# Keeping the low parts of one set of FFN weights in DRAM, made early, in a two-layer recurrent decoder on one core

## The chip, the cores and the metric

The kernel runs on one core of one Trainium2 chip. The metric is the device time of one execution in microseconds (us). The engines are named as in the profile: PE (TensorE matmul), PEld (its weight load, which overlaps the matmuls), DVE (VectorE), ACT (ScalarE), POOL (GpSimd) and SP (SyncE, which here issues nearly all DMAs, in order).

## The reference, cut to what matters

Two layers, each `x = x + mixer(rmsnorm(x))` and then `x = x + swiglu(rmsnorm(x))`, over 1024 prompt rows and 64 sample rows (1088 columns in the kernel). Layer 0's mixer joins an S5 recurrence and a gated delta network, layer 1's mixer is RWKV-7. The change touches the SwiGLU of layer 1 only, with d = 1024 and 2816 hidden columns (22 blocks of 128):

```
def swiglu(h, w_gate, w_up, w_down):
    return (jax.nn.silu(h @ w_gate) * (h @ w_up)) @ w_down
```

Everything is float32. The kernel gets close to float32 from three faster products: a weight `w` is split into a rounded high part `wh` and a low part `wl = w - wh`, the activation likewise into `hi` and `lo`, and each block computes `wh*hi + wh*lo + wl*hi` (helper `mm`, line 322).

## The kernel before

The columns are worked in two halves (512 and 576 columns), and each half in two chunks (256 or 288 columns). The program is written as: projections and recurrences of layer 0; then for each half layer 0's output projection and FFN 0, followed by the RWKV projections and the RWKV units (eight feature tiles, two time segments each) of that half; then for each half layer 1's output projection and FFN 1. A list scheduler reorders it, engine by engine, so that work from neighbouring stages is interleaved: the RWKV units of the first half run beside FFN 0 of the second half, and the RWKV units of the second half run beside FFN 1 of the first half. The FFN 1 of the second half has nothing beside it.

An FFN (`ffn`) goes through 22 hidden blocks. For each block it makes the gate product and the up product (PSUM tiles `pg`, 24 matmuls for a chunk, two PSUM banks in turn), forms the activation (`s`, `ah`, `al`: lines 510 to 519) and, for every three blocks, runs the down product: eight output tiles, each two chunks of nine matmuls into `pd`, which DVE adds to the residual (line 534). The next output tile needs a new 128x384 weight.

Every weight comes through the helper `weight` (lines 295 to 312 of the listing below): SP loads it from DRAM into one of two `raw` buffers, ACT rounds it into `wh` (line 305), and the low part is made by a subtraction (line 309) on POOL, or on DVE where the caller says so. The FFN's down weights use DVE in the stages that have no RWKV beside them (`alone`). A weight of class `Kept` is different: the first time its low part is also stored to a DRAM copy (line 311), and from then on (`there`) the low part is loaded (line 307) and no subtraction is made. Before the change the layer-0 FFN weights and the projections are `Kept`; the layer-1 FFN weights `wg`, `wup` and `wd` are not, so that FFN 1 makes its low parts twice, once for each half.

The pools that matter: `raw` has two buffers, `wh` and `wl` three, `wdh` and `wdl` two. Memory on the right side of the scratchpad is first layer 0's and, after `right.close()`, that of the RWKV constants and work tiles.

Of the kernel before, what the change touches and what calls it, by code (L numbers as in the profile page):

```python
# [8 lines left out]
F32 = mybir.dt.float32  # L9
F32R = mybir.dt.float32r  # L10
# [15 lines left out]
NF = D_FF // 128  # L26
# [78 lines left out]
class Kern:  # L105
# [188 lines left out]
    def weight(self, src, kt=8, m=128, tag="w", bufs=3, lo=None):  # L294


        nc = self.nc
        kept, src = (src, src.src) if isinstance(src, Kept) else (None, src)
        raw = self.dp.tile([128, 1024], F32, tag="raw", name="raw", bufs=2)
        raw = raw[:, :kt * m].rearrange("p (k m) -> p k m", m=m)  # L300
        nc.sync.dma_start(raw, src)
        p = self.dx if tag == "wd" else self.dp
        wh = p.tile([128, kt, m], F32R, tag=tag + "h", name=tag + "h", bufs=bufs)
        wl = p.tile([128, kt, m], F32R, tag=tag + "l", name=tag + "l", bufs=bufs)
        nc.scalar.copy(wh, raw)  # L305
        if kept and kept.root.there:
            nc.sync.dma_start(wl.bitcast(F32), kept.low)
            return wh, wl
        (lo or nc.gpsimd).tensor_sub(wl, raw, wh)  # L309
        if kept:  # L310
            nc.sync.dma_start(kept.low, wl.bitcast(F32))
        return wh, wl

    def mm(self, ps, w, x, cn, c=0):

        his, los = x
        wt = [[a[:, k] for k in range(len(his))] if not isinstance(a, list) else a for a in w]
        last = 3 * len(his) - 1
        i = 0
        for k, (xh, xl) in enumerate(zip(his, los)):  # L320
            for a, b in ((wt[0], xh), (wt[0], xl), (wt[1], xh)):
                self.nc.tensor.matmul(ps, a[k], b[:, c:c + cn], start=i == 0, stop=i == last)  # L322
                i += 1
# [1557 lines left out]
def mixed0(K, s, dyg, dy, wglu):  # L1881


    nc = K.nc
    v = nc.vector
    t0, W, chunks = HALF[s]
    kn = W // 8
    cn = 4 * kn
    gs = [K.hilo(4) for i in range(2)]
    ys = []  # L1890
    for m in range(4):
        t = K.ring("act", "yg")[:, :W]
        nc.sync.dma_start(t.rearrange("p (s k) -> p s k", s=8), dyg[m][:, :, 64 * s:64 * s + kn])
        ys.append(t)
        for i, (gh, gl) in enumerate(gs):
            y = t[:, cn * i:cn * i + cn]
            nc.scalar.activation(gh[m][:, :cn], y, AF.Copy, scale=0.5)
            v.scalar_tensor_tensor(gl[m][:, :cn], y, 0.5, gh[m][:, :cn], op0=OP.mult, op1=OP.subtract)
    hs = [([], []), ([], [])]
    for m in range(4):  # L1900
        w = K.weight(wglu[m], 4)
        for a in hs:
            h, l = K.hilo(1)
            a[0].extend(h)
            a[1].extend(l)
        for i in range(2):
            ps = K.pa("pgl")[:, :cn]
            K.mm(ps, w, gs[i], cn)
            t = K.tmp("gt")[:, :cn]
            nc.scalar.activation(t, ps, AF.Tanh, scale=0.5)  # L1910
            v.scalar_tensor_tensor(t, t, 1.0, ys[m][:, cn * i:cn * i + cn], op0=OP.add, op1=OP.mult)
            t3 = t.rearrange("p (s k) -> p k s", k=kn)
            for c in range(2):
                tc = t3[:, kn // 2 * c:kn // 2 * (c + 1)]
                oh, ol = (x[m][:, :cn].rearrange("p (k s) -> p k s", s=8)[:, :, 4 * i:4 * i + 4] for x in hs[c])
                nc.scalar.activation(oh, tc, AF.Copy, scale=0.25)
                v.scalar_tensor_tensor(ol, tc, 0.25, oh, op0=OP.mult, op1=OP.subtract)
    return [tuple(a + b for a, b in zip(x, y)) for x, y in zip(hs, loaded(K, s, dy))]


def loaded(K, s, dy, own=None):

    t0, W, chunks = HALF[s]
    hs = [([], []) for c in chunks]
    for i, y in enumerate(dy):
        t = K.ring("act", "yr")[:, :W]
        e = own is not None and i == len(dy) - 1
        n = W - own.shape[-1] if e else W
        K.nc.sync.dma_start(t[:, :n], y[:, t0:t0 + n])
        for (c, cn), (h, l) in zip(chunks, hs):  # L1930
            (a,), (b,) = K.hilo(1)
            m = min(max(n - c, 0), cn)
            if m:
                K.split(a[:, :m], b[:, :m], t[:, c:c + m], K.nc.gpsimd if i % 2 else None)
            if m < cn:
                K.split(a[:, m:cn], b[:, m:cn], own[:, c + m - n:c + cn - n])
            h.append(a)
            l.append(b)
    return hs


ORDER = ((0, 1), (2, 3))


@with_exitstack
def trunk(ctx, tc, *aps):
    nc = tc.nc
    I = dict(zip(IN_NAMES, aps))
    I.update({"o_" + n: a for (n, _), a in zip(OUTS, aps[len(IN_NAMES):])})
    K = Kern(ctx, tc)  # L1950
    K.nv = K.const.tile([128, 4, 8], F32, name="nv")
    dr = ctx.enter_context(tc.tile_pool(name="tkd", bufs=1, space=DRAM))
    dx = dr.tile([128, 8, T], F32, name="dx")
    dyr = [dr.tile([128, T], F32, name="dyr%d" % i) for i in range(8)]

    both = ["wglu", "wout", "w1", "a1", "g1", "wk", "wr", "wv", "wo"]
    for n in both:
        I[n] = Kept(I[n], dr.tile(list(I[n].shape), F32, name="low_" + n))
    for n in ("wg", "wup", "wd"):
        I[n] = [Kept(I[n][0], dr.tile(list(I[n].shape[1:]), F32, name="low_" + n)), I[n][1]]  # L1960
    right = ctx.enter_context(ExitStack())
    dyg, dy, second, early = layer0(K, I, right, dr)
    K.open(ctx, 288, 4, reuse_waits="tile")

    def tail(s, src, ys, w, i, x=None, done=None, ahead=lambda: None):
        if early is not None and s == i == 0:
            early.close()
            K.open_more(ctx, reuse_waits="tile")
        x = K.load_x(src, s, x)
        first = s == i == 0  # L1970
        ready = {}

        def gate():
            ready[0, 0] = K.weight(I["wg"][i][0])

        norms = K.project(x, ys, HALF[s][2], w, (lambda: None) if first else gate, 7 if first else 8)
        if first:
            second(ORDER[0])
            with tc.high_priority(3000):
                norms = K.project_last(x, ys, HALF[s][2], w, gate)  # L1980
            second(ORDER[1])
        return x, K.ffn(x, s, norms, K.nv[:, 1 + i], I["wg"][i], I["wup"][i], I["wd"][i], ready, ahead, s == i, done)

    rw = None
    for s in range(2):
        t0, W, chunks = HALF[s]
        wk0 = []
        keys = lambda: wk0.append(K.weight(I["wk"][0]))
        keep = lambda m, c, cn, t: nc.sync.dma_start(dx[:, m, t0 + c:t0 + c + cn], t)
        x, norms = tail(s, I["x"], mixed0(K, s, dyg, dy, I["wglu"]), I["wout"], 0, done=keep, ahead=keys)  # L1990
        if rw is None:
            right.close()
            rw = RWKV(K, ctx, I["rvec"])
            rw.open(ctx)
        unit = lambda ft, si=2 * s: rw.start(ft, si, I["rs0"], I["o_rwkv"], dyr)
        rw.projections(s, x, I["rsh"], *(I[n] for n in ("w1", "a1", "g1", "lw2", "wk", "wr", "wv")), unit, norms, wk0[0])
        for ft in range(8):
            own = unit(ft, 2 * s + 1)
        for w in [I[n] for n in both[:-1]] + [I[n][0] for n in ("wg", "wup", "wd")]:
            w.there = True  # L2000
    nc.sync.dma_start(I["o_shift"], rw.shift)
    for s in range(2):
        t0, W, chunks = HALF[s]
        I["wo"].there = s > 0
        if s:
            K.psn = rw.norm_bank
        x, (bc, r1) = tail(s, dx, loaded(K, s, dyr, own if s else None), I["wo"], 1, rw.spare() if s else None)
        with tc.issue_after(K.last.ins) if s else ExitStack():
            for i, (c, cn) in enumerate(chunks):
                K.rms([t[:, c:c + cn] for t in x], K.nv[:, 3], K.spread(r1) if i else bc,  # L2010
                      lambda k, t: nc.sync.dma_start(I["o_y"][:, k, t0 + c:t0 + c + cn], t), True,
                      ((1, 3, 5, 7), (5, 7))[i] if s else ())
# [95 lines left out]
```

## Time and profile before

| | us |
|---|---|
| median of three runs | 3722.46 (3709.42 to 3722.55) |
| the profiled execution, its own time | 3726.54 |
| its span in the profile | 3724.8 |
| PE busy | 3456.1 (93%) |
| DVE busy | 2377.6 (64%) |
| ACT busy | 1393.8 (37%) |
| POOL busy | 1041.9 (28%) |
| mean granted TensorE clock | 0.944 |

Busy times are unions of an engine's instructions. Matmuls overlap (one of 256 columns is shown with some 0.28 us, and the next starts 0.12 us later), so a busy PE only says that a matmul was under way. A wait is put down to what ended it. The profile's rows call the stages by time: FFN 0 of the first half runs to about 1100 us, FFN 0 of the second half from 1455 to 2130, FFN 1 of the first half from 2440 to 3200, and FFN 1 of the second half from 3225 to 3700.

### The profile page before, as it was taken

To read this page: it belongs to the slowest core of one execution; us is meant where nothing else is said; L and a number is where in the kernel's file an instruction comes from. 1 tells how busy PE (TensorE), PEld (TensorE's weight loads), DVE (VectorE), ACT (ScalarE), POOL (GpSimd) and SP (SyncE) were. 2 spreads that over 40 slices of the span, in tenths; PEclk is the share of its full clock that TensorE was granted. 3 is DMA by queue.
4 is the path that set the end of the run, shared out by engine and by line. 5 is a ranking of instruction groups with operands and counts; after the bars stand their busy time and mean duration, and the time that the engine had idled before them with its cause. 6 is when DMAs were issued, how large, how long until landed. Compare 5 with 4: busy or idle time off the path is not lost. (4 is left out here: it accounts for less than half of the span.)

```text
span 3724.8 us, 77416 instructions
## 1 busy us (share of the span) xinstructions
PE 3456.1 (93%) x29894; PEld 3211.8 (86%) x29894; DVE 2377.6 (64%) x6834; ACT 1393.8 (37%) x3264; POOL 1041.9 (28%) x1037
## 2 busy tenths in 40 slices
PE   7889999999998889999999988899999999899998
PEld 6879888899987788899999887888888878899997
DVE  6976888654456456766666663467787877453444
ACT  3333333322224444444444344444344433322222
POOL 3322233222316441211111042233343333132221
PEclk8989987999997899899999989999999999999999
DMA  4424453445554584344443435832233322522322
GB/s 102 96 84 129 96 176 93 143 144 174 188 173 125 172 275 149 110 142 141 140 151 117 137 117 176 281 127 60 81 94 93 91 70 84 179 74 72 94 80 66
DMA packets 387552, 474.36 MB, mean 127 GB/s; under 512 B 142312, under 2 KB 305896, under 8 KB 387184
## 3 DMA queue, kind: packets, MB, share of 16 engines
q1 hardware_dynamic: 377968, 460.51, 40.5%
q10 hardware_dynamic: 9216, 8.92, 0.7%
q8 instruction: 235, 3.85, 0.4%
q14 instruction: 133, 1.09, 0.1%
HBM read 344.32 MB, written 123.79 MB: 126 GB/s over the span
## 5 line engine op out<-in xcount | busy, mean ns | idle before, releaser
L322 PE MATMUL pg<-hi,wh 128*128 128x288 f32 (+1 forms) x2816 | 836.2, 297 | 17.8 <-DVE s L511 14.6
L322 PE MATMUL pg<-lo,wh 128*128 128x288 f32 (+1 forms) x2816 | 833.4, 296 | 5.7 <-DVE lo L409 4.7
L322 PE MATMUL pg<-hi,wl 128*128 128x288 f32 (+1 forms) x2816 | 831.5, 295 | 1.1 <-POOL wl L309 1.0
L309 POOL TENSOR_TENSOR wl<-raw,wh 128x1024 fp32r<-128x1024 f32 (+3 forms) x205 | 480.4, 2347 | 924.0 <-ACT wh L305 864.6
L322 PEld LDWEIGHTS pg<-hi,wh 128*128 128x128 f32 x2816 | 540.4, 192 | 29.8 <-DVE s L511 17.6
L322 PEld LDWEIGHTS pg<-lo,wh 128*128 128x128 f32 x2816 | 540.7, 192 | 13.5 <-DVE lo L409 6.3
L322 PEld LDWEIGHTS pg<-hi,wl 128*128 128x128 f32 x2816 | 540.7, 192 | 5.4 <-POOL wl L309 1.5
L305 ACT CAST wh<-raw 128x1024 fp32r<-128x1024 f32 (+3 forms) x309 | 312.8, 1013 | 394.6 <-PE pg L322 88.0
L322 PE MATMUL pd<-ah,wdh 128*128 128x256 f32 (+1 forms) x1280 | 385.2, 301 | 20.8 <-DVE x L534 15.1
L322 PE MATMUL pd<-ah,wdl 128*128 128x256 f32 (+1 forms) x1280 | 370.6, 290 | 0.6 <-DMA wdl<-low_wd 0.4
L322 PE MATMUL pd<-al,wdh 128*128 128x256 f32 (+1 forms) x1280 | 369.9, 289 | 0.0
L322 PEld LDWEIGHTS pd<-ah,wdh 128*128 128x128 f32 x1280 | 241.6, 189 | 30.6 <-DVE x L534 17.2
L322 PE MATMUL pj<-hi,wh 128*128 128x256 f32 (+1 forms) x768 | 243.3, 319 | 21.0 <-ACT st L1400 10.1
L322 PE MATMUL pj<-lo,wh 128*128 128x256 f32 (+1 forms) x768 | 243.2, 317 | 15.1 <-DVE lo L409 12.8
L322 PE MATMUL pj<-hi,wl 128*128 128x256 f32 (+1 forms) x768 | 238.5, 313 | 11.4 <-DMA wl<-low_wr 6.9
L322 PEld LDWEIGHTS pd<-ah,wdl 128*128 128x128 f32 x1280 | 241.5, 189 | 3.4 <-DMA wdl<-low_wd 1.3
L322 PEld LDWEIGHTS pd<-al,wdh 128*128 128x128 f32 x1280 | 242.0, 189 | 0.6
L534 DVE TENSOR_TENSOR x<-x,pd 128x256 f32<-128x256 f32 (+1 forms) x384 | 162.8, 427 | 96.3 <-PE pd L322 92.5
L305 ACT CAST wdh<-raw 128x384 fp32r<-128x384 f32 (+1 forms) x224 | 111.2, 497 | 258.4 <-PE pd L322 161.2
L322 PE MATMUL pi<-hi,wh 128*128 128x272 f32 x640 | 191.5, 299 | 3.1 <-ACT us L1809 1.5
L322 PE MATMUL pi<-lo,wh 128*128 128x272 f32 x640 | 190.4, 297 | 0.0
L322 PE MATMUL pi<-hi,wl 128*128 128x272 f32 x640 | 190.1, 297 | 0.0
(643 smaller groups left out, 8066.3 us busy)
## 6 DMA issues: line engine op xcount, KB each, us to landing
raw<-in_wg SPq DMA_DIRECT2D x88, 512.0 KB
raw<-in_wup SPq DMA_DIRECT2D x88, 512.0 KB
raw<-in_wd SPq DMA_DIRECT2D x192, 192.0 KB
low_wg<-wl SPq DMA_DIRECT2D x22, 512.0 KB
low_wup<-wl SPq DMA_DIRECT2D x22, 512.0 KB
wl<-low_wg SPq DMA_DIRECT2D x22, 512.0 KB
wl<-low_wup SPq DMA_DIRECT2D x22, 512.0 KB
raw<-in_win SPq DMA_DIRECT2D x20, 512.0 KB
```

The lines of the kernel that those rows point to most:

```text
L305: nc.scalar.copy(wh, raw)
L309: (lo or nc.gpsimd).tensor_sub(wl, raw, wh)
L322: self.nc.tensor.matmul(ps, a[k], b[:, c:c + cn], start=i == 0, stop=i == last)
L534: v.tensor_add(x[m][:, c:c + cn], x[m][:, c:c + cn], ps)
```

## The change

The gate weights of layer 1 (`wg`, 22 tiles of 128x1024, 512 KB each) become `Kept` too. A new helper `keep` goes through them once: it loads a tile into `kraw`, rounds it on ACT into `kwh`, subtracts on DVE into `kwl`, and stores `kwl` to DRAM. It uses one buffer of each kind, from a pool on the right side that is open between layer 0's close and the opening of the RWKV pools, and it stands in the program behind FFN 0 of the first half. FFN 1 then loads `wl` for its gate weights in both halves. Up and down weights of layer 1 stay as they are.

```diff
+    def keep(self, pool, w, n):
+
+        nc = self.nc
+        for i in range(n):
+            raw, wh, wl = (pool.tile(list(w[i].src.shape), t, tag=n, name=n, bufs=1)
+                           for n, t in (("kraw", F32), ("kwh", F32R), ("kwl", F32R)))
+            nc.sync.dma_start(raw, w[i].src)
+            nc.scalar.copy(wh, raw)
+            nc.vector.tensor_sub(wl, raw, wh)
+            nc.sync.dma_start(w[i].low, wl.bitcast(F32))
+        w.there = True
...
+FIRST = ('wg',)
...
     for n in ("wg", "wup", "wd"):
-        I[n] = [Kept(I[n][0], dr.tile(list(I[n].shape[1:]), F32, name="low_" + n)), I[n][1]]
+        I[n] = [Kept(I[n][i], dr.tile(list(I[n].shape[1:]), F32, name="low%d_%s" % (i, n)))
+                if i == 0 or n in FIRST else I[n][i] for i in range(2)]
...
         if rw is None:
             right.close()
+            with tc.tile_pool(name="keep", bufs=1, side="right") as kp:
+                for n in FIRST:
+                    K.keep(kp, I[n][1], NF)
             rw = RWKV(K, ctx, I["rvec"])
             rw.open(ctx)
```

In all the built program has 22 more loads (`kraw`), 22 more stores (`kwl`) and 44 more loads (`wl<-low_wg`) on SP, 22 more casts on ACT, 22 more subtractions on DVE and 44 fewer subtractions on POOL; the matmuls are the same in number.

Where `keep` goes is seen on DVE, in FFN 0 of the first half, at a down product. Before (an `x` row is the addition of a `pd` chunk to the residual, `wdl` the low part of a down weight):

```order
L519 SCALAR_TENSOR_TENSOR al<-s,ah 128x256
L534 TENSOR_TENSOR x<-x,pd 128x256 x2
L309 TENSOR_TENSOR wdl<-raw,wdh 128x384
L534 TENSOR_TENSOR x<-x,pd 128x256 x2
L309 TENSOR_TENSOR wdl<-raw,wdh 128x384
L534 TENSOR_TENSOR x<-x,pd 128x256 x2
L309 TENSOR_TENSOR wdl<-raw,wdh 128x384
L534 TENSOR_TENSOR x<-x,pd 128x256 x2
L309 TENSOR_TENSOR wdl<-raw,wdh 128x384
```

The same place now (line 546 is what was line 534, and 531 what was 519):

```order
L322 TENSOR_TENSOR kwl<-kraw,kwh 128x1024
L531 SCALAR_TENSOR_TENSOR al<-s,ah 128x256
L546 TENSOR_TENSOR x<-x,pd 128x256 x2
L309 TENSOR_TENSOR wdl<-raw,wdh 128x384
L546 TENSOR_TENSOR x<-x,pd 128x256 x2
L309 TENSOR_TENSOR wdl<-raw,wdh 128x384
L546 TENSOR_TENSOR x<-x,pd 128x256 x2
L322 TENSOR_TENSOR kwl<-kraw,kwh 128x1024
L309 TENSOR_TENSOR wdl<-raw,wdh 128x384
L546 TENSOR_TENSOR x<-x,pd 128x256 x2
```

Three new subtractions stand between this row of `al` and the end of this down product. Of the 22, seven stand among or right behind the additions of a down product and fifteen among the gate and up products; the first stands beside what ran at 851 us before, the last beside 1026 us.

On SP, at the same place, a row of before:

```order
L301 DMA raw<-in_wd 128x384
L311 DMA low_wd<-wdl 128x384
L301 DMA raw<-in_wd 128x384
L311 DMA low_wd<-wdl 128x384
L301 DMA raw<-in_wd 128x384
L311 DMA low_wd<-wdl 128x384
L301 DMA raw<-in_wd 128x384
```

And now:

```order
L301 DMA raw<-in_wd 128x384
L323 DMA low_wg<-kwl 128x1024
L320 DMA kraw<-in_wg 128x1024
L311 DMA low_wd<-wdl 128x384
L301 DMA raw<-in_wd 128x384
L311 DMA low_wd<-wdl 128x384
L301 DMA raw<-in_wd 128x384
L323 DMA low_wg<-kwl 128x1024
L320 DMA kraw<-in_wg 128x1024
```

A store that waits for DVE and a load of 512 KB come in for every two loads of a down weight. The loads of the RWKV constants (`rvec`), which stood right behind layer 0, now stand behind the last `kwl` store, as their memory is the pool's.

On POOL, at the start of FFN 1 of the first half, before (`yc`, `AR`, `BK`, `XV`, `H`, `Hs` belong to the RWKV units):

```order
L1713 TENSOR_TENSOR yc<-yc,rs 128x256
L309 TENSOR_TENSOR wl<-raw,wh 128x1024 x4
L1601 TENSOR_TENSOR AR<-rkb,P 64x4x64
L309 TENSOR_TENSOR wl<-raw,wh 128x1024
L1693 COPY Hs<-H 128x64
L1669 COPY XV<-Hs 64x64 x2
L1667 COPY H<-Hs 128x64
L309 TENSOR_TENSOR wdl<-raw,wdh 128x384
L1609 TENSOR_TENSOR BK<-kp,Pi 64x4x64 x2
L309 TENSOR_TENSOR wl<-raw,wh 128x1024
```

And now:

```order
L1725 TENSOR_TENSOR yc<-yc,rs 128x256
L309 TENSOR_TENSOR wl<-raw,wh 128x1024 x2
L1613 TENSOR_TENSOR AR<-rkb,P 64x4x64
L309 TENSOR_TENSOR wl<-raw,wh 128x1024
L309 TENSOR_TENSOR wdl<-raw,wdh 128x384
L1705 COPY Hs<-H 128x64
L1681 COPY XV<-Hs 64x64 x2
L1679 COPY H<-Hs 128x64
L309 TENSOR_TENSOR wdl<-raw,wdh 128x384
L1621 TENSOR_TENSOR BK<-kp,Pi 64x4x64 x2
```

Two of the four subtractions are gone there; what is left in FFN 1 are those of the up and down weights. The scheduler has also moved other instructions against each other in all stages where an FFN and RWKV units are interleaved; each pair of units still ends within some 85 of the FFN's matmuls from where it ended before.

## Rows read from the trace of the kernel before

**Rows 1.** The page's first part: engine, busy us, share of the span, instructions.
```profile
PE 3456.1 (93%) x29894; PEld 3211.8 (86%) x29894; DVE 2377.6 (64%) x6834; ACT 1393.8 (37%) x3264; POOL 1041.9 (28%) x1037
```

**Rows 2.** Busy time by stretch: length, PE, PEld, DVE, ACT, POOL, clock, DMA share, GB/s.
```profile
1455.00:2130.00 675.00, 666.17 (x6138) 612.05 (x6141) 442.59 (x1609) 281.13 (x738) 75.31 (x132) 0.98 0.44 132
2440.00:3200.00 760.00, 705.58 (x7135) 627.15 (x7135) 595.88 (x1858) 312.87 (x852) 273.86 (x262) 0.96 0.31 93
3225.00:3700.00 475.00, 465.53 (x3571) 459.73 (x3569) 200.04 (x380) 124.80 (x219) 112.80 (x52) 0.98 0.25 78
```

**Rows 3.** PE's waits in 2440 to 3200: us in total, times, longest.
```profile
PE pd L322 <- DVE x L534: 12.2, 14, 4.6
PE pg L322 <- DVE s L511: 9.5, 9, 1.9
PE pc L1678 <- ACT X L1677: 7.2, 5, 2.9
```

**Rows 4.** POOL's weight subtractions in 2440 to 3200 by shape: busy us, mean ns.
```profile
L309 POOL TENSOR_TENSOR wl<-raw,wh 128x1024 fp32r<-128x1024 f32 x48 | 115.5, 2410 | 123.1 <-ACT wh L305 110.5 <-PE po L322 4.4 <-PE pc L1678 2.3
L309 POOL TENSOR_TENSOR wdl<-raw,wdh 128x384 fp32r<-128x384 f32 x48 | 50.0, 1043 | 91.5 <-ACT wdh L305 77.8 <-DMA k<-dk 6.2 <-DMA raw<-in_wd 2.5
L309 POOL TENSOR_TENSOR wdl<-raw,wdh 128x256 fp32r<-128x256 f32 x8 | 5.8, 730 | 29.9 <-PE py L1689 15.8 <-ACT wdh L305 12.5 <-PE pd L322 1.6
```

**Rows 5.** Tile T in 1455 to 2130, then in 2440 to 3200: ns min/median/max.
```profile
L188 DVE TENSOR_TENSOR T<-T,Tm x210: 153/196/723, 1468.8 to 2067.4; 32x15 f32<-32x15 f32 x14, 32x39 f32<-32x39 f32 x14, 32x55 f32<-32x55 f32 x14, 32x63 f32<-32x63 f32 x14
L188 DVE TENSOR_TENSOR T<-T,Tm x225: 154/201/2432, 2440.0 to 3131.0; 32x15 f32<-32x15 f32 x8, 32x39 f32<-32x39 f32 x8, 32x55 f32<-32x55 f32 x8, 32x63 f32<-32x63 f32 x8
```

**Rows 6.** Order of time, 895 to 901, DVE and POOL: start, us, instruction.
```profile
898.92 2.40 DVE L519 SCALAR_TENSOR_TENSOR al<-s,ah 128x256 fp32r<-128x256 f32 x1 [0.90 <-ACT ah L518]
...
898.65 2.40 POOL L309 TENSOR_TENSOR wl<-raw,wh 128x1024 fp32r<-128x1024 f32 x1 [0.46 <-ACT wh L305]
```

**Rows 7.** Busy time by stretch, where keep will stand, and at the DMA's busiest.
```profile
845.00:1030.00 185.00, 182.02 (x1527) 181.28 (x1526) 82.50 (x170) 52.11 (x93) 53.55 (x27) 1.00 0.55 179
2325.00:2400.00 75.00, 66.33 (x466) 61.89 (x466) 29.70 (x58) 35.51 (x76) 17.85 (x26) 1.00 0.92 312
```

**Rows 8.** DVE's subtraction of a 128x1024 tile (tile wl), ns min/median/max.
```profile
L309 DVE TENSOR_TENSOR wl<-raw,wh x6: 1224/1226/1226, 1093.5 to 3687.6; 128x1024 fp32r<-128x1024 f32 x6
```

**Rows 9.** DVE by line in 845 to 1030: busy us, mean ns, idle before.
```profile
L534 DVE TENSOR_TENSOR x<-x,pd 128x256 f32<-128x256 f32 x51 | 21.3, 420 | 18.0 <-PE pd L322 17.3
L309 DVE TENSOR_TENSOR wdl<-raw,wdh 128x384 fp32r<-128x384 f32 x27 | 15.1, 558 | 9.7 <-ACT wdh L305 9.3
```

**Rows 10.** Busy time by stretches of 12 us in FFN 0 of the first half.
```profile
866.00:878.00 12.00, 12.00 (x104) 12.00 (x103) 6.14 (x14) 2.80 (x6) 0.00 (x0) 1.00 0.37 116
890.00:902.00 12.00, 12.00 (x103) 12.00 (x102) 4.57 (x7) 3.50 (x6) 6.68 (x3) 1.00 0.72 228
926.00:938.00 12.00, 11.14 (x94) 10.97 (x94) 6.38 (x15) 2.05 (x4) 0.00 (x0) 1.00 0.61 180
```

**Rows 11.** ACT by line in 845 to 1030.
```profile
L305 ACT CAST wh<-raw 128x1024 fp32r<-128x1024 f32 x21 | 22.0, 1048 | 41.7 <-PE pg L322 18.8 <-DMA raw<-in_wup 9.6 <-DMA raw<-in_wg 7.3
L305 ACT CAST wdh<-raw 128x384 fp32r<-128x384 f32 x27 | 13.9, 513 | 37.1 <-PE pd L322 18.9 <-DMA raw<-in_wd 18.2
...
L510 ACT ACTIVATE s<-pg 128x256 f32<-128x256 f32 x22 | 8.4, 381 | 15.7 <-PE pg L322 15.6
```

**Rows 12.** Waits in 845 to 1030: PE, then SP's queue.
```profile
PE pd L322 <- ACT wdh L305: 2.0, 2, 1.1
...
SPq L311 <- POOL wl L309: 82.3, 20, 7.7
SPq L311 <- DVE wdl L309: 40.7, 22, 5.7
```

**Rows 13.** PE's waits in 3200 to 3724, those within the FFN.
```profile
PE pd L322 <- ACT wh L305: 2.1, 2, 1.3
PE pg L322 <- DVE s L511: 1.5, 1, 1.5
```

## The prediction

> **What bounds the kernel now.** PE is busy 93% of the span [rows 1], so I look only for time in which PE waits. The table by stretch gives it by stage [rows 2]. FFN 1 of the second half (3225 to 3700) has PE busy 465.5 of 475 us, FFN 0 of the second half 666.2 of 675: nothing to win there. FFN 1 of the first half (2440 to 3200) is the one FFN stage with a hole: 705.6 of 760, 54.4 us idle, at a granted clock of 0.96. Its twin, FFN 0 of the second half, also has RWKV units beside it, but loads its low parts: 8.8 us idle, clock 0.98. So I ask what makes the first half's FFN 1 different. DVE is busy 596 of 760 us there against 443 of 675, and POOL 274 against 75 [rows 2]. PE's longest waits are for DVE: the residual additions, 12.2 us, and `s`, 9.5 us [rows 3].
>
> Why DVE is slow there is seen in single rows. The small operations of the RWKV inverse take 0.2 us in the middle of both stages, but up to 2.43 us where POOL subtracts weights, against at most 0.72 us where it does not [rows 5]. And when `al` meets a weight subtraction on POOL, it lasts exactly as long as that one, 2.40 us, and ends with it [rows 6]. DVE, with two operands in the scratchpad, stands still until POOL is done. In the mean DVE spends 596/1858 = 0.321 us on an instruction there and 443/1609 = 0.275 us in the twin stage; with the twin's mean the 1858 would take 511 us, so that about 85 us of DVE are such holding.
>
> **The change part by part.**
>
> *FFN 1, first half (the gain).* 22 of POOL's subtractions go: 22 x 2.41 = 53 us of the 115.5 + 50.0 + 5.8 = 171.3 us of weight subtractions in the stage [rows 4], or 31%. Of the 85 us of holding DVE gets back 26 (bounds: nothing, if the rest of POOL's work moves into the freed time; 53, if each was held all along). What PE gets of it: its idle time over the twin's is 54.4 - 8.8 x 760/675 = 44.5 us, and 31% of that is 14 us. The clock: 0.04 x 760 = 30 us of granted cycles are missing against 0.02 x 675 in the twin, 15 us for the length; 31% is 5 us. So 19 us, between 0 (the rest of the idle time is the units' own chain) and 60 (44.5 + 15, all of it). The 22 loads of `wl` that replace them add 11.5 MB to a stage with a DMA share of 0.31 [rows 2]; I cost them at nothing, since it stays under 0.4 and the twin lives with 0.44.
>
> *FFN 1, second half.* The other 22 subtractions go too, but PE waits in the FFN only 3.6 us, for ACT and for a DVE row [rows 13]. I count nothing; the cover is PE itself, which is full. The 22 loads lie in a DMA share of 0.25.
>
> *The keep stage (the cost).* 22 tiles between about 845 and 1030 us, where PE is busy 182 of 185 us at full clock [rows 7]. Three things are charged there.
>
> First, DVE: a subtraction of a 128x1024 tile takes 1.226 us [rows 8]. Among the additions of a down product, nine matmuls of 0.118 us (12 us hold some 102 of them [rows 10]) fill a bank in 1.06 us; of that DVE needs 0.42 for the addition and half of 0.56 for a `wdl` [rows 9], which leaves 0.36 us. A `kwl` in there makes PE late by 1.226 - 0.36 = 0.87 us; seven of them: 6 us (bounds 0 and 7 x 1.23 = 9).
>
> Second, the fifteen among gate and up products. There a bank lasts 24 x 0.118 = 2.83 us, minus 0.38 for the activation [rows 11] and for `s` about what an addition takes, 0.42 [rows 9]: 2 us to spare, more than 1.226. Only where POOL holds the `kwl` first, for up to 2.4 us, are 3.6 us too many, by 1.6. POOL is busy 29% of the time there (53.55 of 185 [rows 7]); half of the worst in 29% of fifteen is 3 us (bounds 0 and 15 x 1.6 = 24).
>
> Third, the DMAs. 22 x 2 x 0.524 MB = 23.1 MB. The busiest stretch moved 312 GB/s at a share of 0.92 [rows 7], so the engines would do 339, and one tile transfer takes 1.55 us of them, all 44 take 68 us: the share goes from 0.55 to 0.92. That stretch had PE busy only 88% of the time, though for more than one reason. A down weight's cast now waits for its load as often as for PE (18.2 us against 18.9 [rows 11]), and at the end of each down product PE waits already (926 to 938: 94 matmuls for 103 [rows 10]; 1.1 us for `wdh` [rows 12]). The loads are just in time, with about a microsecond of slack from the second buffer of `wdh`. SP adds to it: it is in order and stands 123 us of the 185 at stores that wait for low parts [rows 12]; the new stores wait for `kwl` and hold the next loads of `raw` behind them. With two transfers of 1.55 us at each of the seven tiles of the down products, 22 us are the most that those loads come late. I take half, 11 us, since the slack covers the first microsecond of each. Bounds: 0, and 68 if no transfer were hidden anywhere. ACT's 22 casts of 1.05 us [rows 11] are free where ACT is busy 52 of 185; they hurt only when their load is late, which is in the 11.
>
> *Moved.* The RWKV constants come after the last `kwl`, some 70 us before FFN 0 ends and RWKV needs them: nothing. If keep ran 70 us late, they would be late next, and the whole RWKV half with them. The reshuffled interleaving in the two mixed stages, up to 85 matmuls or 10 us of PE either way for a pair of units, I cost at nothing and widen the range by it.
>
> **The sum.** 6 + 3 + 11 - 19 = +1 us: no change. On the profiled execution's 3726.5 us that is 3727.5; the median of the runs lies 4 us lower, so 3723. Half a per cent, 18.6 us, is about what a measurement of this kernel can tell from no change.
>
> **The rivals.**
>
> *Faster: the keep stage is hidden.* If the loads keep ahead, the cost is the 6 us on DVE, and if the units get more from a freer POOL than its share (POOL's queue also holds RWKV's rows behind a subtraction that waits for ACT, 110.5 us of such waits [rows 4]), the gain is nearer 30. That gives 3699. For it: PE stayed full at a DMA share of 0.72 [rows 10]. Against: 0.92 is not 0.72. Chance 0.30.
>
> *Slower: the DMAs cannot carry keep.* Place: the down products between 850 and 1030 us. If the down weights land later than a weight is used up (18 matmuls, 2.13 us, with two buffers), each of the 27 in the stage [rows 11] is late by a transfer, 1.55 us: 42 us in place of 11, so 3754. It decides once a load of 192 KB takes some microsecond longer than now. For it: casts already wait for loads, SP is blocked two thirds of the time. Against: the average stays under 1, and the tiles come one at a time. Chance 0.18.
>
> *The gain isn't there.* PE's waits for `X`, `XV` and `x` may be the units' own chain, which POOL's rows do not shorten; then only the cost is left, 20 us, 3743. For it: PE is in order, and the third wait in length is for ACT's `X` [rows 3]. Against: the twin stage with the same chain and 8.8 us. Chance 0.10.
>
> *The lock in the keep stage.* If the fifteen are all held by POOL as `al` was [rows 6], they cost 24 us in place of 3, 3744. POOL subtracts there for the same gate and up products that the `kwl` stand between. Chance 0.04. The Trainium skill (SBUF — State Buffer, section Who interferes with whom) states this as a rule: a DVE instruction with two SBUF inputs contends with a GpSimd instruction that reads SBUF, one blocks the other fully, and issue order decides which. Rows 5 and 6 agree, 0.2 against 2.4 us; it speaks for the gain in FFN 1 and against `keep`, which puts a two-input subtraction on DVE beside POOL's.
>
> **How the numbers follow.** The forecast of no change has 0.38. Of it 0.03 and 0.04 fall beyond half a per cent, faster and slower, by the reshuffling. Of the faster rival 0.24 of its 0.30 lies beyond; of the DMA rival 0.16 of 0.18; of the last two 0.09 of 0.14. Faster 0.27, slower 0.29, same 0.44. The range reaches to the faster rival with 10 us of reshuffling, 3690, and to the DMA rival's 3754: 3755; about 0.1 is left out on each side.
>
> **What would show it.** In 2440 to 3200: POOL down by some 50 us, DVE by 26, the largest T row still near 2.4 but fewer of them, PE idle 40 rather than 54. In 845 to 1030: DMA share near 0.9, PE's matmuls thinner by 20 us, waits for `wdh` and behind `kwl`. FFN 1 of the second half unchanged with `al` shorter. Wrong would be: the keep stage as dense as before (then faster), or stretched by 40 us or more (then slower), or FFN 1 of the first half as long as before with POOL at 220 us.

## The result and the profile after

The changed kernel takes **3745.2 us** (median of 4 runs) against 3719.0 of the kernel before (4 runs beside it): ratio 1.0057, 95% interval 1.0035 to 1.0079. (The two medians alone are 26 us, 0.7%, apart.) It is slower by a little over half a per cent, inside the range that was forecast, 22 us above the likeliest value.

The time by stage says where. The stages are cut by PE's own instructions: "keep stage" is from the first to the last matmul into `pd` in FFN 0 of the first half (keep stands in the later part of it); "RWKV 1" from there to one matmul of the output projection ahead of FFN 0 of the second half (the 768th into `po`, the same one in every kernel), "FFN 0, 2nd" to that FFN's last `pd`; "RWKV 2" (to the 1152nd `po`) and "FFN 1, 1st" likewise; "rest" is what follows. All are us, of one profiled execution each; for every other kernel the difference from before is given. e1 to e12 are the experiments below.

| kernel | start | keep stage | RWKV 1 | FFN 0, 2nd | RWKV 2 | FFN 1, 1st | rest | span |
|---|---|---|---|---|---|---|---|---|
| before | 712.2 | 400.9 | 352.6 | 663.9 | 338.0 | 726.0 | 531.2 | 3724.8 |
| after | -0.3 | +25.6 | +6.9 | -3.4 | +12.0 | -17.3 | -3.4 | +20.1 |
| e1 keep alone | -0.2 | +19.5 | +4.4 | -3.3 | +8.7 | -3.1 | -0.7 | +25.3 |
| e2 loads alone | +0.9 | -3.8 | -1.1 | -5.2 | +2.8 | -19.1 | -4.8 | -30.3 |
| e3 no subtraction | +6.2 | +21.1 | +0.3 | -5.0 | -0.6 | -21.6 | -1.3 | -0.9 |
| e4 DMAs alone | -2.5 | +16.6 | -1.2 | -2.6 | -1.5 | -34.0 | -3.0 | -28.2 |
| e5 other order | -0.4 | +29.0 | -1.9 | -3.3 | +4.7 | -33.2 | -2.9 | -8.0 |
| e6 two buffers | -2.8 | +23.8 | +2.8 | -3.2 | +3.8 | -18.4 | -1.5 | +4.5 |
| e7 POOL subtracts | +1.5 | +38.9 | -1.5 | -1.5 | +4.3 | -37.0 | -1.5 | +3.2 |
| e8 stores by ACT | -2.6 | +31.6 | -3.1 | -5.4 | +1.1 | -13.3 | -5.4 | +2.9 |
| e9 DMAs by POOL | +4.4 | +31.7 | +1.3 | -0.2 | -4.2 | -36.8 | -2.7 | -6.5 |
| e10 half the tiles | +1.4 | +14.5 | -1.8 | -1.1 | +0.8 | -10.6 | -3.7 | -0.5 |
| e11 gate low on DVE | -2.2 | +1.6 | -3.6 | -0.8 | +2.8 | -31.6 | +0.2 | -33.6 |
| e12 gate, up on DVE | +5.9 | -1.8 | +0.4 | -5.3 | +5.6 | -54.4 | +6.3 | -43.3 |

The first column holds no edited work (up to 712 us all these programs do the same), and yet runs from -2.8 to +6.2. The changed kernel and e1 run the same instructions in the same order on every engine for the first 2500 us, and yet are 6.1 us apart in the keep stage and 11.7 at the end of RWKV 2. So one reading of a stage is good to about 6 us, and only what repeats, or is larger, is taken as a finding below. (In "FFN 0, 2nd" all twelve differences are negative: it is before's own reading that is some 3 us long.) Whole executions of one kernel differ too: the profiled one of before took 3726.5 us, 7.5 over its kernel's median, that of e3 3725.7, 18 over, and one of e10's twelve, 4588 us at a granted clock of 0.64, is left out of its figures.

Busy time by those stages, answering [rows 2, 7] (columns: PE, PEld, DVE, ACT, POOL, granted clock, DMA share, GB/s): before, the keep stage, RWKV 2 and FFN 1 of the first half,

```profile
712.20:1113.10 400.90, 387.31 (x3273) 375.30 (x3271) 200.28 (x477) 109.65 (x210) 98.69 (x52) 0.97 0.51 167
...
2129.60:2467.60 338.00, 294.26 (x2184) 273.47 (x2183) 177.12 (x450) 157.36 (x353) 119.03 (x162) 0.91 0.58 187
2467.60:3193.60 726.00, 675.04 (x6778) 599.41 (x6776) 573.27 (x1768) 298.74 (x819) 264.27 (x256) 0.96 0.30 88
```

and in the changed kernel all five, keep stage to FFN 1 of the first half:

```profile
711.90:1138.40 426.50, 398.82 (x3272) 382.39 (x3271) 221.55 (x496) 131.66 (x232) 98.30 (x52) 0.96 0.63 211
1138.40:1497.90 359.50, 303.68 (x2313) 281.45 (x2312) 210.72 (x472) 167.37 (x396) 162.84 (x180) 0.89 0.57 181
1497.90:2158.40 660.50, 649.86 (x6049) 597.62 (x6047) 435.21 (x1576) 276.98 (x725) 70.66 (x127) 0.99 0.44 133
2158.40:2508.40 350.00, 298.84 (x2182) 276.69 (x2182) 176.90 (x445) 157.32 (x353) 118.98 (x161) 0.90 0.56 180
2508.40:3217.10 708.70, 665.50 (x6778) 594.87 (x6776) 536.00 (x1769) 297.05 (x819) 209.60 (x234) 0.97 0.35 107
```

In the last row PE is idle 43.2 us, the clock is 0.97, and POOL is down to 209.6 us; before has 51.0, 0.96 and 264.3. PE's two longest waits in the stretch answer [rows 3]; line numbers above 312 are 12 higher than before:

```profile
PE pd L334 <- DVE x L546: 11.7, 17, 1.8
PE pg L334 <- DVE s L523: 7.9, 5, 2.9
```

POOL's weight subtractions there, by shape, answer [rows 4]:

```profile
L309 POOL TENSOR_TENSOR wl<-raw,wh 128x1024 fp32r<-128x1024 f32 x23 | 55.5, 2412 | 87.2 <-ACT wh L305 87.0
L309 POOL TENSOR_TENSOR wdl<-raw,wdh 128x384 fp32r<-128x384 f32 x48 | 49.3, 1031 | 91.6 <-ACT wdh L305 86.0 <-PE pt L1642 3.6 <-DMA raw<-in_wd 0.7
```

And tile T, ns min/median/max, answers [rows 5]:

```profile
L188 DVE TENSOR_TENSOR T<-T,Tm x210: 155/200/2417, 2526.5 to 3160.1; 40x15 f32<-40x15 f32 x8, 40x39 f32<-40x39 f32 x8, 40x55 f32<-40x55 f32 x8, 40x63 f32<-40x63 f32 x8
```

Half of the `wl` subtractions are gone (45 before in this cut), and the largest T row is still as long as one that is left. In the keep stage there are new waits. From 844 to 1056 us, around keep, PE, ACT and SP's queue waited thus [rows 11, 12]:

```profile
PE pd L334 <- ACT wdh L305: 4.5, 4, 2.9
PE pd L334 <- DVE s L529: 4.1, 2, 2.9
PE pd L334 <- DVE x L546: 3.9, 5, 1.5
PE pg L334 <- DVE s L523: 1.8, 3, 0.7
PE pd L334 <- DVE wdl L309: 1.6, 2, 0.8
PE pd L334 <- DVE s L523: 1.4, 2, 1.3
...
ACT kwh L321 <- DMA kraw<-in_wg: 27.2, 18, 3.9
...
ACT wdh L305 <- DMA raw<-in_wd: 13.3, 10, 4.6
...
SPq L323 <- DVE al L531: 16.5, 4, 5.5
...
SPq L323 <- DVE kwl L322: 13.1, 5, 4.8
```

The busy times of the same stretch, and keep's casts and subtractions by tile (ns min/median/max):

```profile
844.00:1056.00 212.00, 194.24 (x1544) 189.25 (x1543) 108.06 (x197) 74.66 (x117) 52.72 (x27) 0.98 0.79 268
```
```profile
L321 ACT CAST kwh<-kraw x22: 1044/1050/1056, 848.6 to 1044.9; 128x1024 fp32r<-128x1024 f32 x22
L322 DVE TENSOR_TENSOR kwl<-kraw,kwh x22: 1208/1225/2577, 849.7 to 1046.0; 128x1024 fp32r<-128x1024 f32 x22
```

ACT stands 27.2 us at casts of keep whose load has not landed, with the casts of the weights behind them, and SP stands at keep's stores (line 323). Most `kwl` rows are not held: their median is the bare 1.225 us of [rows 8]. The DMA share is 0.79, PE's busy time 194 of 212 us, the clock 0.98 where it was 1.00 [rows 7]. Of PE's 17.3 us of waits 12.8 end with a row of DVE (0.9 before) and 4.5 with `wdh`.

So the forecast's two large terms are there in nearly their sizes, and a third is there that it had at nothing: the two stretches of RWKV projections, where the change edits nothing, 6.9 + 12.0 us longer, one of them over a thousand us after keep has ended. In RWKV 2 PE is idle 51.2 us in place of 43.7.

### The profile page after: what moved, and what is told of

It reads as the page before. It is cut to its first block, busy times and chain, and to the rows that moved or that the text cites. A ratio compares the mean times of both kernels' runs of the same rounds, so it can differ in the third digit from the quotient of the medians.

```text
span 3744.9 us, 77600 instructions
## 1 busy us (share of the span) xinstructions
PE 3452.8 (92%) x29894; PEld 3207.2 (86%) x29894; DVE 2337.3 (62%) x6856; ACT 1416.5 (38%) x3286; POOL 933.3 (25%) x993
## 4 chain that ended last, share of the span: by engine, by line
PE 62%; DVE 19%; DMA 11%; issue 3%; ACT 3%; POOL 1%; SPq 1%; DVEq 0%; ACTq 0%; POOLq 0%
PE pg L334 24%; PE pd L334 11%; PE po L334 5%; PE pj L334 5%; PE pi L334 3%; DVE Tm L186 1%; DVE T L188 1%; PE pg L1653 1%; PE py L1702 1%; PE pc L1693 1%; DMA raw<-in_wg 1%; DMA raw<-in_wup 1%; DVE mx L1362 1%; DMA kraw<-in_wg 1%; DMA raw<-in_wd 1%
## 5 line engine op out<-in xcount | busy, mean ns | idle before, releaser
L309 POOL TENSOR_TENSOR wl<-raw,wh 128x1024 fp32r<-128x1024 f32 (+3 forms) x161 | 374.5, 2329 | 965.7 <-ACT wh L305 874.2
L334 PE MATMUL pj<-lo,wh 128*128 128x256 f32 (+1 forms) x768 | 245.2, 320 | 19.1 <-DVE lo L421 14.7
L523 DVE SCALAR_TENSOR_TENSOR s<-s,pg 128x288 f32<-128x288 f32 (+1 forms) x176 | 76.2, 433 | 191.4 <-ACT s L522 190.4
```

The lines of the kernel that those rows point to most:

```text
L523: v.scalar_tensor_tensor(t, t, 1.0, ps, op0=OP.add, op1=OP.mult)
```

## The experiments

**e1 and e2: the cost alone, the gain alone.** e1 keeps into a DRAM copy that nobody reads. e2 keeps nothing, and FFN 1 loads layer 0's low parts.

```diff
+    made = {n: Kept(I[n][1], dr.tile(...)) for n in FIRST}       # e1
-                    K.keep(kp, I[n][1], NF)
+                    K.keep(kp, made[n], NF)
```
```diff
+        I[n] = [first, Kept(I[n][1], first.low) if n in FIRST else I[n][1]]   # e2
-                    K.keep(kp, I[n][1], NF)
+                I[n][1].there = True
```

Expected of e1: 

> The cost without the gain: the 22 low parts are made beside FFN 0 of the first half and stored, but FFN 1 makes its own as before. My theory (the change buys about 17 us in FFN 1 of the first half and pays about 25 in the keep stage): FFN 0 of the first half 25 us longer, FFN 1 as in the kernel before, in all 3719 + 25 = 3744 us, and the RWKV projections of the second half, which were 12 us longer in the changed kernel, as before. Rival 1 (those 12 us come from keep, through the moved constants or the reshuffled interleaving): 3756. Rival 2 (the gain was never there, the 17 us are an accident of interleaving): 3745, with FFN 1 of the first half about as short as in the changed kernel.

Expected of e2: 

> The gain without the cost: nothing is kept, and FFN 1 loads as low parts of its gate weights those that layer 0 has left in DRAM (so the low parts are those of other weights; the same bytes move). My theory: FFN 0 of the first half as before, FFN 1 of the first half 17 us shorter, its second half up to 3 shorter, 3719 - 17 = 3702 us. Rival 1 (the 12 us in the RWKV projections belong to the loads and the order they bring): 3714. Rival 2 (the gain isn't there): 3719.

Measured: e1 3751.7 us, ratio 1.0105 (1.0086 to 1.0124); e2 3701.0, ratio 0.9957 (0.994 to 0.9974). The loads alone bring 18 us, in FFN 1 of the first half: as forecast, and PE's matmuls stand in exactly the order of before up to 16 us into it. Keep alone costs 33 us: 19.5 in its stage and 13 in the RWKV projections, so the latter belong to keep's presence, not to the loads (rival 1 of e1). By the medians the two make 33 - 18 = 15 against 26 us, by the ratios 1.0105 + 0.9957 - 1 = 1.0062 against 1.0057: within the intervals they add up to the result.

**e3 and e4: which part of keep costs.** e3 leaves out the subtraction and stores the rounded high part, e4 leaves out the cast as well and stores what it loaded.

```diff
-            nc.vector.tensor_sub(wl, raw, wh)
-            nc.sync.dma_start(w[i].low, wl.bitcast(F32))
+            nc.sync.dma_start(w[i].low, wh.bitcast(F32))     # e3; e4: raw, and no nc.scalar.copy
```

Expected of e3: 

> The changed kernel with keep's 22 subtractions on DVE left out; the rounded high part is stored where the low part was (so FFN 1's gate low parts are wrong), all DMAs and casts stay. My sum gave DVE 9 of 20 us: FFN 0 of the first half 9 us shorter than in the changed kernel, 3745 - 9 = 3736. Rival 1 (DVE is covered; the cost is the DMAs and the queues that wait in order): 3745. Rival 2 (DVE, held by POOL, is all of the cost): 3745 - 25 = 3720.

Expected of e4: 

> The changed kernel with keep's 22 casts on ACT and 22 subtractions on DVE left out: each tile is loaded and stored as it is (low parts wrong), the 44 DMAs stay. My sum gave the DMAs 11 us and ACT nothing: FFN 0 of the first half 11 to 16 us longer than before, 3736, like the run without the subtraction. Rival 1 (ACT, which stood 27 us waiting for keep's loads with the weights' casts behind it, carries the cost): 3720 to 3725, well below the run without the subtraction. Rival 2 (bandwidth carries it all): 3745.

Measured: e3 3707.8 us, ratio 0.998 (0.9964 to 0.9995); e4 3704.9, ratio 0.9962 (0.9947 to 0.9977). By the totals the subtraction alone would be worth 29 us (ratios) to 37 (medians), more than it lasts (22 x 1.225 = 27). The stages say otherwise: in the keep stage e4 is 16.6 longer, e3 21.1, after 25.6, so 17 for the DMAs and some 4 each for casts and subtractions, the latter two within the spread of a reading. The rest is in stages without any keep instruction: no loss in RWKV 1 and 2, and in e4 twice the gain in FFN 1. Taking out instructions had let the scheduler put others elsewhere: that became the next theory. The waits in the trace of e4, between 840 and 1031 us, show what DMAs alone do, on ACT, on SP's queue and on PE:

```profile
ACT wdh L305 <- DMA raw<-in_wd: 39.6, 16, 4.4
...
SPq L320 <- DMA kraw<-in_wg: 46.8, 20, 5.3
SPq L319 <- DMA low_wg<-kraw: 31.8, 19, 5.9
...
PE pd L331 <- DVE x L543: 4.8, 4, 1.9
PE pd L331 <- ACT wdh L305: 3.0, 2, 2.3
```

The down weights' casts wait twice as long for their loads as before (18.2 us, [rows 11]), and SP stands 79 us at keep's own transfers (lines 319 and 320). PE itself waits 3.0 us for `wdh`, against 2.0 before [rows 12], and longer for `x`; so late casts are not shown to be all of the 17 us. In e3, between 850 and 1020 us, they are most of PE's 12.9 us of waits, and DVE ends 2.1:

```profile
PE pd L333 <- ACT wdh L305: 10.8, 6, 3.4
```

**e5: the same instructions in another order.** Keep gets a higher priority in the scheduler, nothing else.

```diff
+                with tc.high_priority(3000):
                   for n in FIRST:
                     K.keep(kp, I[n][1], NF)
```

Expected: 

> The changed kernel with the same instructions, where keep has a higher priority in the scheduler. Beside keep itself this gives the two mixed stages and the RWKV projections nearly the order of the kernel before: 8644 of 8940 matmuls from the end of FFN 0 of the first half to the end of FFN 0 of the second stand in the same place as before, 4514 in the changed kernel. My theory now: keep costs some 22 to 26 us while it runs, and the 7 + 12 us that both stretches of RWKV projections were longer, long after keep, come from the order alone: then 3745 - 19 = 3726 us, with both stretches within 3 us of before. Rival 1 (they come from keep's subtraction in some other way, as the run without it had none): 3745. Rival 2 (the cost is DVE's, and an earlier keep only moves it): 3745, with the same two stretches as before but FFN 0 of the first half longer.

Measured: 3717.6 us, ratio 1.0005 (0.999 to 1.0021): the changed kernel without its loss. It does the same work as the changed kernel, instruction by instruction. The keep stage is no cheaper (+29.0); RWKV 1 and 2 lose 2.8 in place of 18.9, as my theory had it, and FFN 1 of the first half gains 33.2 in place of 17.3, which it had not. Its rows of the keep stage, RWKV 2 and FFN 1:

```profile
711.80:1141.70 429.90, 399.23 (x3273) 383.71 (x3271) 228.44 (x500) 131.59 (x231) 97.88 (x52) 0.96 0.62 210
...
2153.00:2495.70 342.70, 298.31 (x2184) 275.95 (x2183) 175.21 (x450) 157.38 (x353) 120.05 (x162) 0.91 0.56 184
2495.70:3188.50 692.80, 661.70 (x6777) 592.36 (x6776) 528.61 (x1768) 298.12 (x819) 209.66 (x234) 0.98 0.35 109
```

Against the changed kernel's FFN 1, PE is idle 31.1 us in place of 43.2 and the clock is 0.98 in place of 0.97, with POOL's work the same to 0.1 us.

**e6, e7, e8: is it a buffer, the engine, or SP's queue?** Two buffers for each of keep's tiles; the subtraction on POOL; the stores issued by ACT.

```diff
-  ... tag=n, name=n, bufs=1)                          # e6
+  ... tag=n, name=n, bufs=2)
-            nc.vector.tensor_sub(wl, raw, wh)          # e7
+            nc.gpsimd.tensor_sub(wl, raw, wh)
-            nc.sync.dma_start(w[i].low, ...)           # e8
+            nc.scalar.dma_start(w[i].low, ...)
```

Expected of e6: 

> The changed kernel with two buffers for each of keep's three tiles, so that the load of the next tile need not wait for the last store, and ACT finds its tile there. The order of the matmuls is again close to before (8482 of 8940). My theory: the keep stage is 15 us longer for the DMAs and 7 for ACT, which stands in line for a load; the 7 go and the DMAs come closer together, so 15 to 22 us in FFN 0 of the first half, none in the RWKV projections: 3717 to 3724 us. Rival 1 (two tiles in flight crowd the loads of down weights more): FFN 0 of the first half 30 us longer or more, 3732 and up. Rival 2 (DVE): FFN 0 of the first half as in the changed kernel, 25 longer.

Expected of e7: 

> The changed kernel with keep's subtraction on POOL in place of DVE (2.4 us instead of 1.2; POOL is busy 27% there). Order close to before (8329 of 8940). My theory (DVE's subtraction costs PE next to nothing, the DMAs 15 and ACT 7): FFN 0 of the first half 22 us longer than before, as with DVE, or a few more since POOL holds DVE; no loss in the RWKV projections: 3719 + 22 - 18 = 3723. Rival 1 (DVE's subtractions are the cost, and POOL is free): 3705. Rival 2 (POOL holds DVE for 22 x 2.4 us, half of it felt): 3745.

Expected of e8: 

> The changed kernel with keep's stores issued by ACT in place of SP, so that SP no longer stands at a store with the next weight loads behind it; ACT waits for the subtraction instead. Order close to before (8865 of 8940). My theory: if SP's in-order wait is most of the 15 us that the DMAs alone cost, FFN 0 of the first half is 10 us or less longer than before: 3719 + 10 - 18 = 3711. Rival 1 (the bytes are the cost, not the queue): 22 longer, 3723. Rival 2 (ACT in line for DVE holds the casts of the weights): 30 longer or more, 3731 and up.

Measured: e6 3738.4 us (1.0072; 1.005 to 1.0094), e7 3725.1 (1.003; 1.0016 to 1.0045), e8 3738.2 (1.0066; 1.0047 to 1.0086). None makes the keep stage cheap: +23.8, +38.9, +31.6. Two buffers squeeze keep into 118 us, and from 842 to 965 us the DMA engines are as full as in the fullest stretch of before (0.92, [rows 7]):

```profile
842.00:965.00 123.00, 106.21 (x811) 103.15 (x811) 66.51 (x111) 49.09 (x71) 25.79 (x12) 0.94 0.91 327
```

Yet the stage loses what it loses when the tiles come spread over 200 us at a share of 0.79. As far as one reading each can say, it isn't the share that sets the price. With the subtraction on POOL the stage costs 13 us more than with it on DVE in the changed kernel, 10 more than in e5, though POOL has the time: e7's total came out where I expected it, for another reason (38.9 paid, 37.0 gained). In e8 rival 2's figures came out (30 longer or more, 3731 and up). That ACT, in line behind DVE, is a worse place for the stores than SP is not shown: with SP the stage cost 19.5 (e1) to 29.0 (e5).

**e9 and e10: both DMAs by POOL, and half of the tiles.**

```diff
-            nc.sync.dma_start(raw, w[i].src)           # e9, and the store likewise
+            nc.gpsimd.dma_start(raw, w[i].src)
-                    K.keep(kp, I[n][1], NF)            # e10
+                    K.keep(kp, I[n][1], NF // 2)
+                    I[n][1] = [I[n][1][f] if f < NF // 2 else I[n][1].src[f] for f in range(NF)]
```

Expected of e9: 

> The changed kernel with both of keep's DMAs, 22 loads and 22 stores, issued by POOL in place of SP, so that no weight load of SP stands behind them. In FFN 1 of the first half the matmuls stand in exactly the same order (7093 of 7093) as in the run with the DMAs alone and in the run with the higher priority, where that stage was 34 and 33 us shorter than before; in the RWKV projections the order is close to before (8331 of 8940). My theory (order decides a stage's gain, and SP's queue is a good part of keep's cost): FFN 1 of the first half 34 us shorter, RWKV projections within 5 us, FFN 0 of the first half 10 to 15 longer: 3717 - 34 + 12 + 3 = 3698 us, faster than both. Rival 1 (the bytes, ACT and DVE are the cost, not the queue): FFN 0 of the first half 28 longer, 3714. Rival 2 (POOL stands at stores and its own weight subtractions come late): 40 longer, 3725. Rival 3 (the order of the matmuls is not what decides FFN 1): that stage 17 shorter, and the time 15 more in each case.

Expected of e10: 

> The changed kernel with 11 of the 22 gate weights kept; FFN 1 makes the low parts of the other 11 as before. The RWKV projections and FFN 0 of the second half have exactly the order of the kernel before (8940 of 8940 matmuls). My theory (a kept tile costs some 1.1 us wherever it stands, 24 us for 22, and gains 0.8 us in FFN 1; the RWKV projections lose by the order alone): FFN 0 of the first half 12 us longer, RWKV projections within 3 us, FFN 1 of the first half 8 to 17 shorter by its order: 3717 + 12 - 9 = 3720 us. Rival 1 (the cost is a matter of full DMA engines, so that half the tiles in half the time cost as much each, but the tiles of one down product fewer): 3715. Rival 2 (the RWKV projections lose by keep itself): 10 us longer there, 3730.

Measured: e9 3722.7 us (1.0022; 1.001 to 1.0035), e10 3729.5 (median of eleven; 1.0037; 1.0021 to 1.0052). e9's FFN 1, in the order of e4 and e5, gained 36.8, as foretold from the order; its keep stage cost 31.7 and not 12: rivals 1 and 2. POOL now stood in line itself, 848 to 1067 us:

```profile
POOL low_wg L323 <- DVE kwl L322: 111.8, 22, 9.5
```

e10 has the RWKV projections in before's order, and they lose nothing (-1.8, +0.8). Eleven tiles cost 14.5 us, 1.3 each, 22 cost 25.6, 1.2 each; half of the gain was left, 10.6. The median lies 10 us above what I expected, and 3 above the profiled execution; the eleven range from 3718 to 3741, and I have no cause for the 10.

**e11 and e12: the gain without keep.** If FFN 1 loses because POOL's subtractions hold DVE, DVE may as well make them itself, in half the time, from what is there anyway. Both start from the kernel before; nothing is kept or loaded.

```diff
-                ready[f, i] = self.weight((wg, wu)[i][f])
+                ready[f, i] = self.weight((wg, wu)[i][f], lo=v if own and not i else None)   # e11; e12: if own
```
(`own` is true in FFN 1 of the first half alone; its first gate weight is fetched ahead of it and stays with POOL.)

Expected of e11: 

> The kernel before, without keep and without loads of low parts in FFN 1; in FFN 1 of the first half DVE makes the 22 gate low parts in place of POOL, at 1.23 in place of 2.4 us each. Order as before up to FFN 1. My theory (FFN 1 gains because 22 POOL subtractions no longer hold DVE): DVE is held 26 us less and works 27 us more, but POOL's queue is 53 us freer and no single wait is longer than 1.3 us for these; I expect a good half of the 19 us of the loads alone, 10 us: 3716 - 10 = 3706 us, with plus or minus 16 for the order that falls to it. Rival 1 (DVE's total is what counts): no change, 3716. Rival 2 (DVE is nearer the limit than POOL, and its own subtractions stand in front of the RWKV rows): 10 slower, 3726.

Expected of e12: 

> As the run before, with the 22 low parts of the up weights on DVE too, so that POOL subtracts only the down weights in that stage. My theory: twice the step, but DVE then works 54 us for the low parts: 3716 - 15 = 3701 us, with plus or minus 16 for the order. Rival 1 (DVE's total is what counts): 3716. Rival 2 (DVE becomes the limit among the gate and up products): 20 slower, 3736.

Measured: e11 3687.6 us, ratio 0.9927 (0.9915 to 0.994); e12 **3679.3 us, ratio 0.9901 (0.9887 to 0.9915)**, faster than both kernels, and by more than I expected. FFN 1 of the first half, e11 and then e12:

```profile
2465.40:3159.80 694.40, 668.56 (x6777) 597.20 (x6776) 554.41 (x1786) 299.41 (x819) 217.41 (x235) 0.97 0.31 92
```
```profile
2472.40:3144.00 671.60, 649.90 (x6733) 584.47 (x6732) 545.01 (x1796) 296.28 (x814) 161.54 (x211) 0.98 0.31 94
```

In e12, DVE's `wl` rows and tile T in that stretch (ns min/median/max):

```profile
L309 DVE TENSOR_TENSOR wl<-raw,wh x45: 1178/1218/1579, 2497.3 to 3119.4; 128x1024 fp32r<-128x1024 f32 x45
...
L188 DVE TENSOR_TENSOR T<-T,Tm x210: 155/200/1019, 2489.4 to 3099.1; 40x15 f32<-40x15 f32 x8, 40x39 f32<-40x39 f32 x8, 40x55 f32<-40x55 f32 x8, 40x63 f32<-40x63 f32 x8
```

(e12 has moved 44 matmuls from this stage to the next, so that 6 of its 54 us stand again in "rest".) Two of the 45 `wl` rows DVE made before too, so it has 43 x 1.22 = 52 us more to do. It is busy 28 us less than before, 5 of which stand in "rest" with the moved matmuls: by this estimate 52 + 28 - 5 = 75 us of its 573 were standing still. The longest T row is now 1.02 us, beside a row of the units on POOL (`vx`, 1.27 us); one row of `Tm`, the other half of the same recurrence, lasts 2.13 us, from 2854.5, beside three POOL instructions in a row. What share of the 48 us fell to a luckier order I can't tell from these two runs.

## Why the prediction was right in its parts and 22 us off in its middle

- **The gain in FFN 1, first half (19 us forecast): right in the mechanism, in the number partly by luck.** 17.3 in the changed kernel, 19.1 in e2, where all before it stands in the old order. POOL is 55 us down (50 said), DVE 37 (26 said), the T rows are as long as ever but fewer. The split was off: PE's idle time fell by 8 us (51.0 to 43.2) where the sum had 14, and by the clock, 0.96 to 0.97, some 8 us of granted cycles came back (0.04 x 726 against 0.03 x 709) where it had 5. And the same subtractions gone brought 33 to 37 us in e4, e5, e7 and e9 (below): 19 is what the order that this edit drew gives. The estimate of 85 us of holding is near the 75 of e12. (In [rows 6] `al` lasts as long as POOL's subtraction, but starts and ends 0.27 us after it, not with it.) The Trainium skill (SBUF — State Buffer, section Who interferes with whom) has the rule: a DVE instruction with two SBUF inputs and a GpSimd instruction that reads SBUF exclude each other in full. The T rows agree, up to 2.42 us where POOL makes `wl` subtractions, up to 1.02 us where it makes two in the whole stretch (e12).
- **FFN 1, second half (nothing forecast).** All that follows FFN 1 of the first half is 3.4 us shorter, within a reading's spread, though DVE's `al` rows there, as foretold, take less: 21.2 us in all in place of 47.7.
- **The keep stage (20 us forecast): right in size, its shares not separated.** 25.6; the same work gave 19.5 in e1 and 29.0 in e5. The DMAs I had at 11 are 17 (e4). DVE I had at 9 and ACT's casts at nothing; the steps of e3 show some 4 for each, less than two readings of one order differ by. PE's own waits put it otherwise: 12.8 of 17.3 us end with DVE in the changed kernel (11.9 of 16.3 in e1, the same order), 2.1 of 12.9 without the subtraction (e3), where `wdh` has taken their place. So the terms do not add up as my sum had them. Nor is it all idle time: PE's grew by 14.1 us (13.6 to 27.7), and the clock in the stage fell from 0.97 to 0.96, for which the sum had no term. That late loads of down weights are a way in which the DMAs hurt is what the waits of e3 and e4 show; whether SP's queue or the shared DMA engines make them late is not separated. The price per tile, 1.1 us where the share around keep is 0.91 (e6), 0.9 to 1.3 where it is 0.79 to 0.81 (e1, after, e5), and 1.3 for half of the tiles, speaks against the rival in which the engines are too full. The Trainium skill says in the same section that a DMA never contends with a compute engine. ACT's rows agree: `kwh` casts took 1.05 us at a share of 0.79, like the casts of [rows 11] at 0.55 [rows 7]; the DMAs made them wait, not last longer.
- **"The reshuffled interleaving ... I cost at nothing": the step that failed.** It accounts for 18.9 of the 19 us by which the profiled span overshot the sum (+20.1 against +1). By the traces, of the 8354 matmuls between the last `pd` of FFN 0 of the first half and that of the second, 3383 stand in the changed kernel where they stood before, (4514 of 8940 in the wider cut of e5's expectation), and the RWKV projections lose 18.9 us; e1 has that very order and loses 13.1. e2, e10, e11 and e12 have the order of before and lie between -1.0 and +6.0, all eleven others between -2.9 and +6.6. In RWKV 2 PE is idle 51.2 and 49.8 us in the changed kernel and e1, 40 to 47 in the twelve other kernels. e5, same work, order near before's (8239 matmuls): +2.8. It is not a matter of likeness to before alone: e3's order differs as much (2993) and loses nothing. In FFN 1 of the first half two orders can be told apart. e4, e5 and e9 have the matmuls of that stretch in one identical order, and e7 nearly: -34.0, -33.2, -36.8, -37.0, with PE idle 29 to 33 us. e2 and e6 share another, and of its last 7093 matmuls e8 has 7083 in the same place and the changed kernel 6828: -19.1, -18.4, -13.3, -17.3, with PE idle 40 to 44. All of them load as many low parts there. So an order is worth some 16 us in FFN 1 and some 10 to 16 in the RWKV projections, more than the 10 I had widened the range by, and more than the difference between the change's own gain and cost. Shown is that order, with the work held equal, makes the 0.5% between e5 and the changed kernel. Which instruction out of place does it, the runs leave open.
- **The rivals.** "The gain isn't there" falls with e2. "Faster: keep is hidden" falls with e1 and e4. "The DMAs cannot carry keep" gave a time near the result (3754) by a mechanism that isn't there at 42 us. The lock in the keep stage is small for `kwl` on DVE: its median is 1.225 us, and its 22 rows take 30.4 us, 3.4 more than at that length.

## What to carry to other kernels

When a list scheduler orders the program, an edit is also a draw of a new order, everywhere behind it. Compare stages that the edit doesn't touch before believing a total, and try the same instructions under another priority: here that was worth as much as the change. A helper that runs beside a full PE was paid for by the tile, some 1 us for each, though engines and bandwidth had room; the engines that work in order (SP at its stores, ACT at a cast) passed the wait on. And where POOL held DVE, the cheapest cure was to give DVE the work: its busy time fell by doing more.

## What the runs showed of the hardware that was not expected

- DVE took on 52 us of subtractions in e12, and its busy time fell from 573 to 545 us (5 of the 28 moved to the next stage). By the estimate above, the 43 that POOL no longer made had held it for 75 us, 1.7 us of each 2.41.
- For over 100 us the DMA engines ran at a share of 0.91 and 327 GB/s (e6), and a kept tile cost no more, 1.1 us, than at 0.79 (1.2; each good to 0.3).
- No other issuing engine was cheaper: the same 44 DMAs with the same casts and subtractions cost the stage 19.5 to 29.0 us from SP, 31.7 from POOL (which stood 111.8 of 219 us at stores), 31.6 with the stores from ACT.
